# Projecting q and k already transposed, in a two-layer hybrid decoder trunk on one core

## The chip, the cores and the metric

The kernel runs on one NeuronCore of a Trainium2 chip. The metric is device time in microseconds for one execution of the whole program, compared as the median of several executions. The engines are named as the profile names them: PE (TensorE matmul), PEld (its weight loads, which overlap PE), DVE (VectorE), ACT (ScalarE), POOL (GpSimd) and SP (SyncE, which issues the DMAs).

## The reference

Two layers over 512 tokens of width 1024, all in float32. Each layer is

```
h = x + RMSNorm( MixerBlock( RMSNorm(x) ) )
x = h + RMSNorm( ConvGeGLU( RMSNorm(h) ) )
```

One projection `xn @ w_in` feeds three token mixers and their gates. Heads are 64 wide, and the first 16 columns of every q and k head are turned by rotary embedding (column i with column i+8).

- A: dilated window attention, three groups (dilation 1, 4, 16) of 4 heads. Groups 1 and 2 are computed on tokens sorted by residue modulo 4.
- B: 4 heads over the 128 keys that an indexer chooses. The indexer has 8 q heads, one k head and one weight per head: relu(q k), summed with the weights, then top 128 by 16 rounds of eight maxima.
- C: differential attention, 4 heads with two q/k pairs each and values 128 wide.

Each mixer's output is projected to 1024, multiplied by a sigmoid gate, summed, and projected by `w_out`.

## The kernel before, in words

**Numbers.** Every matmul operand is cut into a high and a low part (`split`, line 79: ACT writes the high part, DVE subtracts for the low one), and each product is three matmuls (`mm3`, line 87: lines 88, 89, 90). All weights go through this: `w_emit` (line 112) takes the next unit of a fixed plan, issues its DMAs on SP into a `wr` tile (2 slots) and splits it into `wh` and `wl` (5 slots each). A unit holds at most 1024 elements a partition.

**Order of the work.** `ORDER` (line 44) lists the projection units and gate blocks of a layer. A scheduler orders instructions at compile time by this program order and by its own estimate of time; on the chip each engine runs its list in order. The code lays the attention between the projections by hand: `later(f, lag)` puts a piece of work aside, and `slot()` (line 328) runs what is due, up to two index-score jobs, one step of up to three attention chains in flight (scores, transpose, values), and some steps of top-k. `slot()` is called after each token tile of a projection, and after each gate block.

**The projection unit** (`proj_unit`, line 396) makes q, k and v of two heads (A, B) or of one C head. For each of the four tiles of 128 tokens `proj_tile` (line 370) runs 8 x 3 matmuls: the transposed normed input (`xh`, `xl`, 128 tokens) stands as the weights, and 384 weight columns move (456 in the first unit, which also makes the indexer's k and head weights). Then:

- ACT copies q and k (and v, for groups 1 and 2) out of PSUM into `qr` (line 411);
- DVE applies rotary with four small instructions (`rope`, lines 362 to 365);
- after each second tile PE transposes q and k of two tiles in a group of four transposes (`tqk`, line 437);
- `double_k` (lines 388, 390) and `stack_q` (lines 381 to 384) cut the transposed halves into high and low parts, two heads apart on the partitions, each instruction 64 partitions by 256 tokens;
- v is split out of PSUM. For groups 1 and 2 it goes to DRAM and comes back in residue order (`vr`).

`index_q` (line 705) makes the indexer's q the same way: three tiles, 512 columns moving, four transposes each (line 718). The gate blocks (`branch`, line 752) already stand the weights and move all 512 tokens.

**A layer's start.** The first unit can only project a token tile when `boundary` (line 789) and `pre_norm` (line 221) of the layer before have normed it and PE has transposed it (line 237); the four tiles come one after another.

Of the kernel before, what the change touches and what calls it, by code (L numbers as in the profile page):

```python
# [40 lines left out]
SBUF_SLOTS = dict(u=10, qk=4, v=4, wr=2, wh=5, wl=5, sm=4, pt=4, qr=3, vr=1, th=3, s=24, s1=2, md=4, wi=1, lp=1, q0=2, cw=1)  # L41
# [8 lines left out]
def tile_trunk(ctx, tc, x, positions, w_in, w_br_a, w_br_b, w_br_c, w_out, lam_q1, lam_k1, lam_q2, lam_k2,  # L50
# [88 lines left out]
    def w_ahead(n):  # L139
        w_emit(wnext[0] + n)  # L140
# [5 lines left out]
    unit_cols = {}  # L146
    for g in range(3):
        for p in range(2):
            b = 768 * g + p * P
            unit_cols["A", g, p] = [(b, P), (b + 256, P), (b + 512, P)]  # L150
    unit_cols["A", 0, 0] = unit_cols["A", 0, 0] + [(OFF_I + 512, 72)]
    for h in range(4):
        b = OFF_C + h * P
        unit_cols["C", h] = [(b, P), (b + 512, P), (b + 1024, P)]
    for p in range(2):
        b = OFF_B + p * P
        unit_cols["B", p] = [(b, P), (b + 256, P), (b + 512, P)]
    unit_cols["I"] = [(OFF_I, 512)]
    def plan_unit(l, u):
        cols = unit_cols[u]  # L160
        width = sum(w for _, w in cols)
        for kk in range(4):
            def srcs(rv, kk=kk):
                o = 0
                for c0, w in cols:
                    yield rv[:, :, o:o + w], rows(w_in[l, kk * 256:(kk + 1) * 256, c0:c0 + w])
                    o += w
            w_unit((l, u, kk), [2, width], srcs)
# [17 lines left out]
    def plan_layer(l):  # L186
        for u in ORDER:
            if u[0] in BRANCH:
                plan_branch(l, BRANCH[u[0]], *u[1:])
            else:  # L190
                plan_unit(l, u)
# [120 lines left out]

    xdr = [x[0]] + [dr.tile([S, D], F32, name=f"xd{i}") for i in range(3)] + [out[0]]
    a_scr = [[dr.tile([S, 132], F32, name=f"ascr{l}_{p}") for p in range(2)] for l in range(DEPTH)]
    v_scr = [[[dr.tile([S, P], F32, name=f"vscr{l}_{g}_{p}") for p in range(2)] for g in range(2)] for l in range(DEPTH)]
# [39 lines left out]

    def rope(v, nh, ti):
        t1 = alloc([P, 8, 16], F32, "s1")
        t2 = alloc([P, 8, 16], F32, "s1")
# [18 lines left out]


# [17 lines left out]
    def proj_unit(l, u, perm, nh, idx=None):  # L396


        keys = [(l, u, kk) for kk in range(4)]
        n = sum(w for _, w in unit_cols[u])  # L400
        dv = P // nh
        qkT = alloc([P, 6, S], F32R, "qk")
        v = alloc([P, NT, nh, 2, dv], F32R, "v")
        raws = []
        for t in range(NT):
            units = w_get(keys)
            acc = proj_tile(units, t, n)
            w_ahead(2)
            qr = alloc([P, 384], F32, "qr")
            nq = 384 if perm is not None else 256  # L410
            nc.scalar.copy(qr[:, 0:nq], acc[:, 0:nq])
            if perm is not None:
                nc.sync.dma_start(perm[t * P:(t + 1) * P, :], qr[:, 256:384])
            else:
                vv = acc[:, 256:384].rearrange("p (h d) -> p h d", h=nh)
                split(v[:, t, :, 0, :], v[:, t, :, 1, :], vv)
            nh_r = 4
            if idx is not None:
                nc.scalar.copy(qr[:, 256:320], acc[:, 384:448])
                nc.scalar.activation(idx["w"][:, t, :], acc[:, 448:456], AF.Copy, scale=float(8 ** -0.5))  # L420
                nh_r = 5
            rope(heads(qr[:, 0:nh_r * HD]), nh_r, t)
            if idx is not None:
                nc.vector.tensor_copy(qr[:, 320:384], qr[:, 256:320])
            raws.append(qr)

            def tk(t=t, qr=qr):
                tp = palloc("tp")
                nc.tensor.transpose(tp[:, 0:P], qr[:, 256:384], ident)
                c = slice(t * P, (t + 1) * P)  # L430
                split(idx["k"][:, 0, c], idx["k"][:, 1, c], tp[:, 0:P])

            def tqk(j=t // 2):
                tp = palloc("tp")
                for i in range(2):
                    for w in range(2):
                        nc.tensor.transpose(tp[:, (2 * w + i) * P:(2 * w + i + 1) * P],
                                            raws[2 * j + i][:, w * P:(w + 1) * P], ident)
                if perm is not None:
                    at = lambda i: qkT[:, i].rearrange("p (r i) -> p r i", r=NT)[:, :, j * 64:(j + 1) * 64]  # L440
                    qt, kt = (tp[:, c:c + 256].rearrange("p (i r) -> p r i", r=NT) for c in (0, 256))
                else:
                    at = lambda i: qkT[:, i, j * 256:(j + 1) * 256]
                    qt, kt = tp[:, 0:256], tp[:, 256:512]
                for h in range(2):
                    double_k(at(2 + 2 * h), at(3 + 2 * h), kt, HALF[h])
                stack_q(at(0), at(1), qt)

            if idx is not None:
                later(tk, 2)  # L450
            if t % 2 == 1:
                later(tqk, 2)
            if t < NT - 1:
                slot()
        if perm is not None:
            vr = alloc([P, NT, P], F32, "vr")
            nc.sync.dma_start(vr, perm.rearrange("(i r) c -> i r c", r=NT))

            def tv():
                vv = vr.rearrange("p t (h d) -> p t h d", h=nh)  # L460
                split(v[:, :, :, 0, :], v[:, :, :, 1, :], vv)
            later(tv, 2)
        return qkT, v
# [154 lines left out]

    def chains_b(qkT, v, masks, oTs, i):
# [8 lines left out]
        for parts in PARTS:  # L628
            for h in range(2):
# [17 lines left out]
                def fin():  # L647
# [3 lines left out]
                    to_oT(on, oTs, i)  # L651
# [53 lines left out]
    def index_q(l, qi):  # L705
        keys = [(l, "I", kk) for kk in range(4)]
        for t in range(1, NT):
            units = w_get(keys)
            acc = proj_tile(units, t, 512)
            w_ahead(2)  # L710
            qr = alloc([P, 512], F32, "sm")
            nc.scalar.copy(qr, acc)
            rope(heads(qr), 8, t)

            def go(t=t, qr=qr):
                tp = palloc("tp")
                for b in range(4):
                    nc.tensor.transpose(tp[:, b * P:(b + 1) * P], qr[:, b * P:(b + 1) * P], ident)
                c = slice((t - 1) * P, t * P)
                stack_q(qi[:, 0:8:2, c], qi[:, 1:8:2, c], tp.rearrange("p (b c) -> p b c", b=4))  # L720
            later(go, 2)
            if t < NT - 1:
                slot()
# [89 lines left out]
    for t in range(1, NT):  # L813
        later(first[t], t)
# [225 lines left out]
```

## Time and profile before

| what | us |
|---|---|
| median of 3 runs (1870.73 to 1873.17) | 1872.28 |
| the profiled execution, its own time | 1872.52 |
| its span, first to last instruction | 1870.7 |
| PE busy in it | 1836.4 (98%) |
| DVE busy | 1233.6 (66%) |
| ACT busy | 852.5 (46%) |
| POOL busy | 29.8 (2%) |

The time lies 1.8 us over the span. [...] Layer 0's mixer lies at about 20 to 485 us of the span, its feed-forward part up to about 940 us; layer 1 repeats the pattern.

### The profile page before, as it was taken

Reading aid. Unit: us, or ns where it says so; the run is one execution under the profiler, and the core shown is the slowest. Engines: PE = TensorE matmul, PEld = TensorE weight load, DVE = VectorE, ACT = ScalarE, POOL = GpSimd, SP = SyncE. Lnnn points to the kernel's source line nnn. Section 1 sums busy time; section 2 is a strip of 40 time slices with the busy share of each in tenths; the row PEclk is TensorE's granted clock in tenths of the full one; section 3 lists DMA queues with packets and bytes.
Section 4 is the critical chain, followed back from the end, with each engine's and each line's share of the span. In section 5 each row is a group of like instructions: output and inputs, shape, how many; then the busy total and the mean of one; then the engine's idle time right before and its main releaser. Section 6 shows DMA issues by size and latency. Waiting matters only on the chain.

```text
span 1870.7 us, 26241 instructions
## 1 busy us (share of the span) xinstructions
PE 1836.4 (98%) x9565; PEld 1606.0 (86%) x9565; DVE 1233.6 (66%) x2670; ACT 852.5 (46%) x1668; POOL 29.8 (2%) x53
## 2 busy tenths in 40 slices
PE   7999989999999999999999999899999999999998
PEld 6999979988889888888889999799888898888886
DVE  6798998764546666642378898997645576666332
ACT  5666654453335444432256655545533354444221
POOL 0000000000000000000000000000000000000000
PEclk9999999999999999999999999999999999999999
DMA  5333322232343333323332333232323443332341
GB/s 153 98 80 87 86 74 77 67 105 80 102 151 107 110 105 96 91 101 132 122 113 76 78 100 89 68 80 68 105 81 110 135 136 91 101 102 91 101 149 65
DMA packets 265181, 185.28 MB, mean 99 GB/s; under 512 B 14711, under 2 KB 238299, under 8 KB 265051
## 3 DMA queue, kind: packets, MB, share of 16 engines
q1 hardware_dynamic: 265050, 183.60, 33.5%
q8 instruction: 75, 1.23, 0.3%
q14 instruction: 56, 0.45, 0.1%
HBM read 171.99 MB, written 11.57 MB: 98 GB/s over the span
## 4 chain that ended last, share of the span: by engine, by line
PE 80%; DVE 11%; DMA 3%; issue 2%; ACT 2%; SPq 1%; POOL 0%; DVEq 0%; POOLq 0%; ACTq 0%
PE mm L88 18%; PE mm L89 18%; PE mm L90 18%; PE sc L89 4%; PE sc L88 4%; PE sc L90 4%; PE pv L89 2%; PE pv L88 2%; PE pv L90 2%; DVE wl L82 1%; DVE qk L390 1%; DMA wr<-in_w_in_dram 1%; PE pv L488 1%; PE tp L477 1%; DVE u L746 1%
## 5 line engine op out<-in xcount | busy, mean ns | idle before, releaser
L82 DVE TENSOR_TENSOR wl<-wr,wh 128x1024 fp32r<-128x1024 f32 (+2 forms) x314 | 359.4, 1146 | 351.9 <-ACT wh L81 350.8
L81 ACT CAST wh<-wr 128x1024 fp32r<-128x1024 f32 (+2 forms) x314 | 309.7, 988 | 463.5 <-PE mm L90 135.3
L88 PE MATMUL mm<-xh,wh 128*128 128x512 f32 (+1 forms) x784 | 298.3, 381 | 5.5 <-DVE v L82 4.2
L90 PE MATMUL mm<-xh,wl 128*128 128x512 f32 (+1 forms) x784 | 296.5, 378 | 1.2 <-DVE wl L82 1.2
L89 PE MATMUL mm<-xl,wh 128*128 128x512 f32 (+1 forms) x784 | 296.9, 379 | 0.0
L89 PE MATMUL mm<-wl,xh 128*128 128x384 f32 (+2 forms) x816 | 282.8, 347 | 1.1 <-DVE wl L82 1.1
L88 PE MATMUL mm<-wh,xh 128*128 128x384 f32 (+2 forms) x816 | 281.1, 349 | 2.2 <-ACT wh L81 1.0
L90 PE MATMUL mm<-wh,xl 128*128 128x384 f32 (+2 forms) x816 | 282.6, 347 | 0.0
L88 PEld LDWEIGHTS mm<-xh,wh 128*128 128x128 f32 x784 | 147.8, 188 | 32.8 <-DVE v L82 5.0
L90 PEld LDWEIGHTS mm<-xh,wl 128*128 128x128 f32 x784 | 147.7, 188 | 28.2 <-DVE wl L82 1.6
L89 PEld LDWEIGHTS mm<-xl,wh 128*128 128x128 f32 x784 | 147.8, 188 | 25.9 <-DVE xl L82 0.4
L88 PEld LDWEIGHTS mm<-wh,xh 128*128 128x128 f32 x816 | 153.9, 189 | 8.1 <-ACT xh L81 2.0
L89 PEld LDWEIGHTS mm<-wl,xh 128*128 128x128 f32 x816 | 154.4, 189 | 6.2 <-DVE wl L82 2.5
L90 PEld LDWEIGHTS mm<-wh,xl 128*128 128x128 f32 x816 | 154.3, 189 | 3.9 <-DVE s L226 0.3
L90 PE MATMUL sc<-xh,wl 128*128 128x512 f32 (+1 forms) x272 | 99.3, 365 | 0.0
L89 PE MATMUL sc<-xl,wh 128*128 128x512 f32 (+1 forms) x272 | 99.2, 365 | 0.0
L88 PE MATMUL sc<-xh,wh 128*128 128x512 f32 (+1 forms) x272 | 99.0, 365 | 0.0
L89 PE MATMUL mm<-wl,qk 128*128 128x512 f32 x216 | 85.9, 398 | 0.0
L390 DVE TENSOR_TENSOR qk<-tp,qk 64x256 fp32r<-64x256 f32 x192 | 80.6, 420 | 7.7 <-ACT qk L388 4.8
L88 PE MATMUL mm<-wh,qk 128*128 128x512 f32 x216 | 85.5, 396 | 0.0
L388 ACT CAST qk<-tp 64x256 fp32r<-64x256 f32 x192 | 70.2, 366 | 33.3 <-DVE qk L390 26.1
L90 PE MATMUL mm<-wh,qk 128*128 128x512 f32 x216 | 85.0, 395 | 0.0
(262 smaller groups left out, 3331.7 us busy)
## 6 DMA issues: line engine op xcount, KB each, us to landing
wr<-in_w_ffn_up_dram SPq DMA_DIRECT2D x176, 256.0 KB, 3.4
wr<-in_w_in_dram SPq DMA_DIRECT2D x282, 128.0 KB, 2.4
wr<-in_w_in_dram SPq DMA_DIRECT2D x56, 512.0 KB, 3.8
wr<-in_w_ffn_down_dram SPq DMA_DIRECT2D x44, 512.0 KB, 3.7
wr<-in_w_out_dram SPq DMA_DIRECT2D x16, 512.0 KB, 3.6
xd<-u SPq DMA_DIRECT2D x12, 512.0 KB, 3.1
u<-xd SPq DMA_DIRECT2D x12, 512.0 KB, 6.3
u<-in_x_dram SPq DMA_DIRECT2D x8, 512.0 KB, 6.1
```

The source lines that it names most:

```text
L81: nc.scalar.copy(hi, src)
L82: nc.vector.tensor_tensor(lo, src, hi.bitcast(F32), op=ALU.subtract)
L88: nc.tensor.matmul(dst, a[0], b[0], start=start, stop=False)
L89: nc.tensor.matmul(dst, a[0], b[1], start=False, stop=False)
L90: nc.tensor.matmul(dst, a[1], b[0], start=False, stop=stop)
L388: nc.scalar.copy(kh[o], src[r])
L390: nc.vector.tensor_tensor(kl[o], src[r], kh[r].bitcast(F32), op=ALU.subtract)
L477: nc.tensor.transpose(tp[:, b * P:(b + 1) * P], e[:, b * P:(b + 1) * P], ident)
L488: nc.tensor.matmul(dst, pT[0][:, c], v, start=i == 0, stop=False)
L746: nc.vector.match_replace(out=w, in_to_replace=m8, in_values=w, imm_value=MARK)
```

## The change

- q and k of a unit, and the indexer's q, are made by `proj_block`: a weight block of 128 columns stands, and all 512 tokens move (384 for the indexer's q). The result is already transposed, so lines 437 and 718 go, and with them `qr` and nearly all of `rope`.
- Rotary is done on the transposed result: ACT copies PSUM to `raw`, DVE shuffles partitions within groups of 32 into `swp`, and POOL multiplies `raw` and `swp` by cosine and signed sine tables (two instructions) and adds them (a third). The two tables are built once, with eight transposes.
- `stack_q` and `double_k` now read `raw` from SBUF, 64 partitions by 512 tokens.
- v is projected for many heads at once, in four units: V0 (group 0 of A, with the indexer's k and weights, 328 columns), V1 (groups 1 and 2, 512), V2 (all of C, 512), V3 (B, 256). V1 and V2 are written to DRAM, and each unit loads its 128 columns of it back through `vr` (one slot).
- `ORDER` is new. The eight gate blocks of A come after C1, where before four came after C2 and four after C3.
- `slot()` is called by matmul columns done (`beat`: every 18 x 512), also inside blocks and gate blocks; V units call it once a tile.
- B's final transposes are held back until the last gate blocks. The large `u` tiles have 9 slots, not 10.

The core of the diff:

```diff
-SBUF_SLOTS = dict(u=10, qk=4, v=4, wr=2, wh=5, wl=5, sm=4, pt=4, qr=3, vr=1, ...)
+SBUF_SLOTS = dict(u=9, m1=1, qk=4, v=4, wr=2, wh=5, wl=5, sm=4, pt=4, rp=4, vr=1, ..., kr=2)
-ORDER = [("A", 0, 0), "I", ("A", 1, 0), ("A", 2, 0), ("A", 0, 1), ("A", 1, 1), ("A", 2, 1), ("C", 0), ("C", 1),
-         ("C", 2), ("ga", 0, 4), ("C", 3), ("ga", 4, 8), ("B", 0), ("B", 1), ("gc", 0, 8), ("gb", 0, 8)]
+ORDER = [("V", 0), "I", ("A", 0, 0), ("A", 0, 1), ("V", 1), ("A", 1, 0), ("A", 2, 0), ("A", 1, 1), ("A", 2, 1),
+         ("V", 2), ("C", 0), ("C", 1), ("ga", 0, 8), ("C", 2), ("C", 3), ("V", 3), ("B", 0), ("B", 1),
+         ("gc", 0, 8), ("gb", 0, 8)]
+BEAT = 18 * 512
+    def beat(n):
+        beats[0] += n
+        while beats[0] >= BEAT:
+            beats[0] -= BEAT
+            slot()
+    def proj_block(key, c0=0):
+        w, = w_get([key])
+        n = S - c0
+        acc = palloc("mm")
+        for k in range(KT):
+            mm3(acc[:, 0:n], (w[0][:, k], w[1][:, k]), (xh[:, k, c0:S], xl[:, k, c0:S]), k == 0, k == KT - 1)
+            if k < KT - 1:
+                beat(3 * n)
+        w_ahead(1)
+        raw = alloc([P, S], F32, "rp")
+        swp = alloc([P, S], F32, "rp")
+        nc.scalar.copy(raw[:, 0:n], acc[:, 0:n])
+        nc.vector.stream_shuffle(swp[:, 0:n], raw[:, 0:n], swap)
+        nc.gpsimd.tensor_tensor(raw[:, 0:n], raw[:, 0:n], rot[0][:, c0:S], op=ALU.mult)
+        nc.gpsimd.tensor_tensor(swp[:, 0:n], swp[:, 0:n], rot[1][:, c0:S], op=ALU.mult)
+        nc.gpsimd.tensor_tensor(raw[:, 0:n], raw[:, 0:n], swp[:, 0:n], op=ALU.add)
+        return raw[:, 0:n], 3 * n
-    def proj_unit(l, u, perm, nh, idx=None):
...
+    def v_unit(l, i, vts=None, idx=None):
+        n = sum(w for _, w in v_cols[i])
+        for t in range(NT):
+            acc = proj_tile(w_get([(l, "V", i, kk) for kk in range(4)]), t, n)
+            w_ahead(2)
+            if vts is None:
+                st = alloc([P, S], F32, "rp")
+                nc.scalar.copy(st, acc)
+                nc.sync.dma_start(v_scr[l][i - 1][t * P:(t + 1) * P, :], st)
+            else:
+                for p in range(2):
+                    vv = acc[:, p * P:(p + 1) * P].rearrange("p (h d) -> p h d", h=2)
+                    split(vts[p][:, t, :, 0, :], vts[p][:, t, :, 1, :], vv)
...
+            slot()
+    def qk_unit(l, u, residues=False):
...
+        raw, n = proj_block((l, u, 0))
+        later(lambda raw=raw: stack_q(at(0), at(1), by(raw)))
+        beat(n)
+        raw, n = proj_block((l, u, 1))
+        def dk(raw=raw):
+            for h in range(2):
+                double_k(at(2 + 2 * h), at(3 + 2 * h), by(raw), HALF[h])
+        later(dk)
+        beat(n)
+        return qkT
+    def v_load(l, i, c0, nh):
+        v = v_tile(nh)
+        vr = alloc([P, NT, P], F32, "vr")
...
+        later(tv, 2)
     def index_q(l, qi):
-        for t in range(1, NT):
...
+        for b in range(4):
+            raw, n = proj_block((l, "I", b), P)
+            later(lambda b=b, raw=raw: stack_q(qi[:, 2 * b], qi[:, 2 * b + 1], raw))
+            beat(n)
-                    to_oT(on, oTs, i)
+                    held.append(lambda: to_oT(on, oTs, i))
```

## Rows read from the trace of the kernel before

**Rows 1.** The page: busy us (share, instructions), then DVE busy tenths in 40 slices.

```profile
PE 1836.4 (98%) x9565; PEld 1606.0 (86%) x9565; DVE 1233.6 (66%) x2670; ACT 852.5 (46%) x1668; POOL 29.8 (2%) x53
...
DVE  6798998764546666642378898997645576666332
```

**Rows 2.** The chain that ended last, share of the span by engine.

```profile
PE 80%; DVE 11%; DMA 3%; issue 2%; ACT 2%; SPq 1%; POOL 0%; DVEq 0%; POOLq 0%; ACTq 0%
```

**Rows 3.** Two stretches of layer 0's mixer: us, then each engine's busy us.

```profile
20.00:400.00 380.00, 371.14 (x2186) 346.00 (x2185) 324.52 (x954) 220.12 (x537) 5.44 (x5) 1.00 0.32 82
160.00:250.00 90.00, 88.65 (x562) 85.33 (x561) 82.59 (x264) 52.95 (x139) 0.00 (x0) 1.00 0.32 85
```

**Rows 4.** Timeline of PE around one group of transposes: start us, us, instruction.

```profile
40.28 0.37 PE L90 MATMUL mm<-wh,xl 128*128 128x456 f32 x1
40.49 0.37 PE L88 MATMUL mm<-wh,xh 128*128 128x456 f32 x1
40.70 0.60 PE L437 MATMUL tp<-ident,qr 128*128 128x128 f32 x4
41.05 0.45 PE L89 MATMUL mm<-wl,xh 128*128 128x456 f32 x1
41.34 0.36 PE L90 MATMUL mm<-wh,xl 128*128 128x456 f32 x1
```

**Rows 5.** Groups of transposes by line: count, duration ns min/median/max.

```profile
L437 PE MATMUL tp<-ident,qr x192: 269/273/422, 40.7 to 1322.4; 128*128 128x128 f32 x192
...
L718 PE MATMUL tp<-ident,sm x24: 270/272/296, 58.4 to 995.6; 128*128 128x128 f32 x24
```

**Rows 6.** Timeline of PE: first and last of 7 wide and of 11 narrower matmuls.

```profile
56.64 0.39 PE L90 MATMUL mm<-wh,xl 128*128 128x512 f32 x1
...
58.01 0.40 PE L90 MATMUL mm<-wh,xl 128*128 128x512 f32 x1
...
59.12 0.34 PE L88 MATMUL mm<-wh,xh 128*128 128x384 f32 x1
...
60.86 0.33 PE L89 MATMUL mm<-wl,xh 128*128 128x384 f32 x1
```

**Rows 7.** Timeline of PE at layer 1's start: idle us before, and what ended it.

```profile
952.49 0.47 PE L88 MATMUL mm<-wh,xh 128*128 128x456 f32 x1 [0.25 <-ACT xh L81]
959.22 0.48 PE L88 MATMUL mm<-wh,xh 128*128 128x456 f32 x1 [0.25 <-ACT xh L81]
```

**Rows 8.** Timeline of PE at the first gate blocks of A, layer 0.

```profile
261.29 0.51 PE L88 MATMUL mm<-xh,wh 128*128 128x512 f32 x1 [2.60 <-DVE v L82]
269.55 0.38 PE L488 MATMUL pv<-v,pt 128*128 128x256 f32 x1 [0.82 <-ACT pt L81]
271.24 0.55 PE L477 MATMUL tp<-ident,sm 128*128 128x128 f32 x3 [1.30 <-DVE u L85]
```

**Rows 9.** DVE groups by line and shape: busy us, mean ns of one, idle before.

```profile
L390 DVE TENSOR_TENSOR qk<-tp,qk 64x256 fp32r<-64x256 f32 x192 | 80.6, 420 | 7.7 <-ACT qk L388 4.8
...
L384 DVE TENSOR_TENSOR qk<-tp,qk 64x256 fp32r<-64x256 f32 x48 | 20.4, 426 | 0.9
L383 DVE TENSOR_TENSOR qk<-tp,qk 64x256 fp32r<-64x256 f32 x48 | 20.0, 417 | 4.2 <-ACT qk L382 2.8
L362 DVE TENSOR_TENSOR s<-qr,cc 128x64 f32<-128x64 f32 x88 | 19.3, 219 | 14.0 <-ACT qr L411 13.5
...
L363 DVE TENSOR_TENSOR s<-qr,nsn 128x32 f32<-128x32 f32 x88 | 16.3, 185 | 0.0
...
L781 DVE COPY u<-mm 128x512 f32<-128x512 f32 x12 | 8.3, 691 | 16.0 <-ACT sm L780 16.0
```

**Rows 10.** POOL groups by line and shape: busy us, mean ns of one.

```profile
L256 POOL MEMSET cmask<- 128x512 bf16 x1 | 0.5, 524 | 0.0
...
masks.py:199 POOL TENSOR_SCALAR_AFFINE_SELECT ident<-ident 128x128 f32<-128x128 f32 x1 | 0.3, 292 | 0.0
```

**Rows 11.** Timeline of DVE, 295 to 298 us.

```profile
295.29 1.22 DVE L82 TENSOR_TENSOR wl<-wr,wh 128x1024 fp32r<-128x1024 f32 x1
296.43 0.69 DVE L745 MAX8 s<-u 128x8 f32<-128x512 f32 x1
```

**Rows 12.** Timeline of POOL, the same instruction at two places.

```profile
295.52 1.86 POOL L94 TENSOR_TENSOR s<-s,nhalf 128x4 f32<-128x4 f32 x1 [29.48 <-DVE s L697]
...
325.74 1.01 POOL L94 TENSOR_TENSOR s<-s,nhalf 128x4 f32<-128x4 f32 x1 [28.36 <-DVE s L697]
```

More of the change, by code (lines that the diff above doesn't have):

```diff
@@ L167, in srcs, with plan_qk @@
                     o += w
-            w_unit((l, u, kk), [2, width], srcs)
+            w_unit((l, "V", i, kk), [2, width], srcs)
+    def plan_qk(l, u):
+        for b, col in enumerate(qk_cols[u]):
+            def srcs(rv, col=col):
+                yield rv, rows(w_in[l, :, col:col + P])
+            w_unit((l, u, b), [KT, P], srcs)
     def plan_branch(l, gi, c0, c1):
@@ L394, in score_mm @@
         nc.tensor.matmul(dst, q, kl, start=False, stop=True)
-    def proj_unit(l, u, perm, nh, idx=None):
-        keys = [(l, u, kk) for kk in range(4)]
-        n = sum(w for _, w in unit_cols[u])
-        dv = P // nh
-        qkT = alloc([P, 6, S], F32R, "qk")
[L403 to L463, printed above, removed]
@@ new lines, in v_tile, with tk @@
+    def v_tile(nh):
+        return alloc([P, NT, nh, 2, P // nh], F32R, "v")
+    def v_unit(l, i, vts=None, idx=None):
+        n = sum(w for _, w in v_cols[i])
+        for t in range(NT):
+            acc = proj_tile(w_get([(l, "V", i, kk) for kk in range(4)]), t, n)
[8 more added lines that the diff above has]
+                    split(vts[p][:, t, :, 0, :], vts[p][:, t, :, 1, :], vv)
+            if idx is not None:
+                kr = alloc([P, P], F32, "kr")
+                nc.scalar.copy(kr[:, 0:HD], acc[:, 256:320])
+                nc.scalar.activation(idx["w"][:, t, :], acc[:, 320:328], AF.Copy, scale=float(8 ** -0.5))
+                rope(heads(kr[:, 0:HD]), 1, t)
+                nc.vector.tensor_copy(kr[:, HD:P], kr[:, 0:HD])
+                def tk(t=t, kr=kr):
+                    tp = palloc("tp")
+                    nc.tensor.transpose(tp[:, 0:P], kr, ident)
+                    c = slice(t * P, (t + 1) * P)
+                    split(idx["k"][:, 0, c], idx["k"][:, 1, c], tp[:, 0:P])
+                later(tk, 2)
+            slot()
@@ L814, in tile_trunk @@
         later(first[t], t)
+    later(rotary_rows, 2)
     for l in range(DEPTH):
@@ L861, in tile_trunk @@
                 later(lambda: index_scores(qi, idx["k"], idx["w"], masks), 3)
+            elif u[0] == "V":
+                if u[1] in (0, 3):
+                    vts[u[1]] = [v_tile(2) for _ in range(2)]
+                v_unit(l, u[1], vts.get(u[1]), idx if u[1] == 0 else None)
             elif u[0] == "A":
                 g, p = u[1], u[2]
-                qkT, v = proj_unit(l, u, v_scr[l][g - 1][p] if g > 0 else None, 2, idx if u == ("A", 0, 0) else None)
+                qkT = qk_unit(l, u, g > 0)
+                v = v_load(l, 0, 256 * (g - 1) + p * P, 2) if g > 0 else vts[0][p]
                 if g == 0:
```

95 lines of the change are left out of this document (55 added, 40 removed).

## The prediction

> **What bounds the kernel now.** I read the page first. PE is busy for 98% of the span, DVE for 66%, and DVE's slices show that its share is no average worth using: it is 0.7 to 0.9 in the first eight slices, which are layer 0's mixer, and again from slice 21 on [rows 1]. The chain that ended last lies on PE for 80% of the span and on DVE for 11% [rows 2]. So PE work that goes away is gained almost whole, wherever DVE doesn't step into its place. The stretches say how close that is: from 20 to 400 us PE is idle for 9 us of 380 and DVE for 55.5, and from 160 to 250 us DVE has 7.4 us left of 90 [rows 3]. Two limits lie close together there: PE binds, and DVE could.
>
> **PE: the transposes.** A transpose's recorded 273 ns is no price, since records overlap; the distance between starts is. Around one group of four, matmuls of 456 columns start 0.21 us apart; after the matmul at 40.49 the second next would start at 40.91, and it starts at 41.34 [rows 4]. A group costs 0.43 us. There are 192 transposes of q and k and 24 of the indexer's q [rows 5], that is 54 groups: 54 x 0.43 = 23.2 us. The tables add two groups, 0.9 us.
>
> **PE: wider matmuls.** The columns that move are the same before and after; their number per matmul isn't. Seven matmuls of 512 columns start 1.37 us apart from first to last, 0.228 us each; eleven of 384 take 1.74 us, 0.174 each [rows 6]. That is 0.00042 us a column, and by this line 328 columns take 0.150 and 256 take 0.120. Before, from the loops: 2112 of 384, 192 of 456 and 144 of 512 columns, 367.5 + 40.3 + 32.8 = 440.6 us. After: 1536 of 512, 192 of 384, 192 of 328 and 192 of 256, 350.2 + 33.4 + 28.8 + 23.0 = 435.4 us. That is 5.2 us less. Together with the transposes PE loses 23.2 - 0.9 + 5.2 = 27.5 us.
>
> **A layer's start.** At layer 1's start PE waits for token tiles as they are normed: it idles 0.25 us for `xh` at 952.49 and at 959.22, and the last tile's date is set by DVE, not by PE [rows 7]. Before, three tiles of the first unit, 24 x 0.21 = 5.0 us each, fill the time until the fourth. V0's tile is narrower, 24 x 0.150 = 3.6 us, and nothing else is ready, since the next blocks want all tokens. Three tiles fill 4.2 us less, and that PE stands idle: +4.2 in layer 1, and I take half, +2.1, in layer 0, where loads and not norms set the date. Bounds 0 and 8.4. One `u` slot fewer could make the residual's tile load later; I take 0 for that, since the slots are freed at the pace of the same norms, with 3 us as its bound.
>
> **DVE.** Rotary goes: the instructions of lines 362 and 363, and 365 and 364, which have their shapes and are taken at their price, 88 x 2 x (0.219 + 0.185) = 71 us, with 80.6 + 20.4 + 20.0 us of low parts [rows 9], 192 us in all. Back come 48 shuffles, 96 low parts of k and 48 of q, all 512 wide. The shuffle isn't in this trace; the nearest row, a copy of 128x512, takes 0.69 us [rows 9], and I take it for all three: 192 x 0.69 = 132 us. If the shuffle took twice that, it would be 33 us more. The relief is 60 us, 30 a layer; small instructions overlap their neighbours more than long ones, so I count 25. With the 55.5 us that are free [rows 3], DVE has about 80 us a layer to give. The indexer and C's values come out about even.
>
> **ACT** keeps a like amount: copies of 512 columns for copies of 256, and half as many high parts twice as wide. It is half idle in the stretch [rows 3], so I cost it at nothing. The same holds for SP: one weight DMA a block in place of three a quarter unit, of the same bytes. The load of `vr` is issued behind weights that are several units ahead, and `vr` has one slot, whose former reader is due two slots after its own load and the next load more than five slots later; so no weight DMA should wait behind it.
>
> **POOL.** 28 blocks a layer bring 84 instructions of 512 columns with two inputs. No such instruction is in the trace. The nearest below is a memset of 512 columns, 0.52 us; the nearest that reads is a select on 128 float32 columns, 0.29 us, four times which is 1.17 [rows 10]. Two inputs read in turn would double that, 2.3 us. I take 1.2, by the row that reads, and keep 0.52 and 2.3 as ends. Three of them are 3.6 us, against 24 x 0.228 = 5.5 us of PE for a block: POOL keeps up, with four `rp` buffers and three PSUM banks between. [...]
>
> **What POOL and DVE share.** The same POOL instruction takes 1.01 us at 325.74 and 1.86 us at 295.52; at the second place DVE was inside `wl<-wr,wh`, which reads two SBUF tensors, from 295.29 to 296.51, and POOL ended 0.87 us after that [rows 11, 12]. POOL waits for a DVE instruction of this kind. Whether DVE waits for POOL the trace doesn't show, since POOL's instructions here read 4 columns or fewer. The bounds of what one POOL instruction costs DVE are 0 and its whole length, 1.2 us. I take half, 0.6, because DVE often has an instruction with a PSUM input or one input next: 84 x 0.6 = 50 us a layer, within the 80. In the tightest stretch it is just hidden, so I add 2 us a layer for waits that leak, +4.
>
> **The sum.** Against the profiled execution's 1872.5 us (the median of the runs, 1872.28, is the same): 1872.5 - 27.5 + 6.3 + 4 = 1855 us.
>
> **Rivals.** *Slower: the shared read side makes DVE the bound.* If DVE stands still for each POOL instruction's whole 1.2 us, a layer loses 84 x 1.2 = 101 us against 80 free, 21 us over, 42 in both layers: 1855 - 4 + 42 = 1893 us. DVE becomes the bound from 0.95 us lost an instruction, and the kernel is slower than before from 1.08 (21 us of net gain used up). For it: the wait at 295.52 and DVE's 82.6 of 90 us [rows 3, 12]. Against: much of DVE's work there, top-k and masked scores, has one SBUF input. [...]
>
> *The wait for A grows.* At the first gate blocks of A PE idles 2.60, 0.82 and 1.30 us, on DVE and ACT [rows 8]: A's combined output isn't there yet. Before, 12 slots of projection lie between A's last unit and these gates; now V2 gives 4 and C0 and C1 give 5.3. The 2.7 missing slots are worth 18 x 0.228 = 4.1 us each, 22 us in both layers at most; gate products that need no A output can fill about half. That gives 1855 + 11 = 1866, at worst 1877. My sum has 0 here, as DVE's relief pulls the other way.
>
> *Faster still.* If DVE's relief counts and POOL's share costs nothing, those 4.7 us of waits a layer go, and the leak with them: 1855 - 9.4 - 4 = 1842.
>
> That the transposes stay in another form I exclude: the diff leaves no PE instruction in their place.
>
> **Chances.** About 0.2%, 3.7 us, is what a measurement of this kernel can tell from no change, so faster means below 1868.5 and slower above 1876. The forecast, with 1846 to 1864 as its own range, 0.50; the wait for A, 1864 to 1878, 0.17, half of it faster and a third within; DVE as the bound, 0.20, with its low edge (0.02) within and the rest slower; faster still, 0.13. Faster: 0.50 + 0.13 + 0.08 = 0.71; within 0.2%: 0.06 + 0.02 = 0.08; slower: the rest, 0.21. The range of 8 in 10 leaves out the upper half of DVE as the bound and the lower half of the fastest case: 1840 to 1890.
>
> **What would show it.** Right: no group at lines 437 and 718's place, projections as 512-column matmuls 0.228 us apart, about 168 more POOL instructions of 1 to 1.5 us, DVE busy 40 to 60 us less in sum, a few microseconds of idle PE on `xh` at layer 1's start. Wrong: DVE instructions with two SBUF inputs grown well over 0.69 and 1.22 us, or PE waits on `wl` and `qk` released by DVE or POOL all through the mixer; or idle PE of more than 15 us a layer before A's gate blocks; or POOL instructions over 1.8 us, whereby three exceed a block.

## The result, and the profile after

The kernel after takes 1939.32 us (median of 4 runs, 1937.12 to 1941.74) against 1872.38 (1870.73 to 1873.17) of the kernel before on the same chip: a ratio of 1.0359, 95% interval 1.0341 to 1.0377. It is slower by 67 us, where 1855 us was forecast; the range ended at 1890. The profiled execution took 1941.74 us, its span is 1940.0.

The page after (busy us, share and instructions; then the tenths of PE's granted clock, of DVE and of POOL; then the chain by engine) answers to [rows 1, 2]:

```profile
PE 1844.7 (95%) x9021; PEld 1543.6 (80%) x9021; DVE 1313.1 (68%) x2232; ACT 856.2 (44%) x1458; POOL 295.9 (15%) x223
...
DVE  5989798885446766642389987988855466666432
...
POOL 1714230340000000000034351204300000000000
PEclk9999989999999999999999999899999999999999
...
PE 66%; DVE 18%; ACT 4%; issue 4%; DMA 4%; POOL 3%; SPq 0%; DVEq 0%; POOLq 0%; ACTq 0%
```

The matmuls have become fewer (9565 to 9021), yet PE's busy sum is longer. DVE has 438 instructions less and 80 us more of busy time. The chain has lost 14 points on PE and gained 7 on DVE and 3 on POOL.

The two stretches of [rows 3] (PE, PEld, DVE, ACT, POOL busy, then the granted clock):

```profile
20.00:400.00 380.00, 349.20 (x1753) 293.65 (x1754) 328.37 (x672) 199.92 (x386) 122.62 (x78) 0.94 0.30 84
160.00:250.00 90.00, 83.29 (x425) 69.27 (x425) 78.07 (x147) 54.58 (x98) 31.64 (x18) 0.92 0.30 86
```

PE idles 31 us of 380 where it idled 9, and its granted clock has fallen from 1.00 to 0.94. DVE is as busy as before with 282 instructions less. Layer 0's feed-forward part loses nothing: from 485 to 970 us PE is busy for 484.4 us of 485 at a granted clock of 1.00. So the loss lies in the mixers, and instructions have grown. Which ones, the groups of DVE and POOL show (busy us, mean ns); they answer to [rows 9, 10]:

```profile
L85 DVE TENSOR_TENSOR wl<-wr,wh 128x1024 fp32r<-128x1024 f32 x284 | 356.9, 1258 | 322.0 <-ACT wh L84 321.2
L441 DVE TENSOR_TENSOR qk<-rp,qk 64x512 fp32r<-64x512 f32 x96 | 106.2, 1106 | 13.8 <-ACT qk L439 12.7
L435 DVE TENSOR_TENSOR qk<-rp,qk 64x512 fp32r<-64x512 f32 x24 | 37.1, 1544 | 0.8
L423 DVE STREAM_SHUFFLE rp<-rp 128x512 f32<-128x512 f32 x48 | 35.3, 735 | 0.1
```

```profile
L425 POOL TENSOR_TENSOR rp<-rp,rot 128x512 f32<-128x512 f32 x48 | 82.2, 1713 | 0.0
L424 POOL TENSOR_TENSOR rp<-rp,rot 128x512 f32<-128x512 f32 x48 | 77.8, 1622 | 365.2 <-DVE rp L423 365.2
L426 POOL TENSOR_TENSOR rp<-rp,rp 128x512 f32<-128x512 f32 x48 | 73.7, 1536 | 3.6
```

The shuffle is nearly as priced, 0.735 for 0.69. The low parts of q and k are not: 1.11 and 1.54 us. The timelines show how. First POOL, then DVE, from 60 to 68 us (start, us, instruction); they answer to [rows 11, 12]:

```profile
60.35 1.01 POOL L424 TENSOR_TENSOR rp<-rp,rot 128x384 f32<-128x384 f32 x1
61.32 2.00 POOL L425 TENSOR_TENSOR rp<-rp,rot 128x384 f32<-128x384 f32 x1
63.40 1.21 POOL L426 TENSOR_TENSOR rp<-rp,rp 128x384 f32<-128x384 f32 x1
```

```profile
60.45 1.99 DVE L85 TENSOR_TENSOR wl<-wr,wh 128x1024 fp32r<-128x1024 f32 x1 [0.21 <-ACT wh L84]
62.48 1.26 DVE L434 TENSOR_TENSOR qk<-rp,qk 64x384 fp32r<-64x384 f32 x1
63.77 1.26 DVE L435 TENSOR_TENSOR qk<-rp,qk 64x384 fp32r<-64x384 f32 x1
65.06 1.22 DVE L85 TENSOR_TENSOR wl<-wr,wh 128x1024 fp32r<-128x1024 f32 x1
...
66.83 0.55 DVE L434 TENSOR_TENSOR qk<-rp,qk 64x384 fp32r<-64x384 f32 x1
```

Read them as turns. `wl` begins at 60.45 inside L424, which ends at 61.36, and ends 1.08 us after that. L425, begun at 61.32, ends at 63.32, 0.88 us after `wl` has let go at 62.44. L434, begun at 62.48, ends 0.42 us after L425. At 65.06, with POOL idle, `wl` takes 1.22 us, and at 66.83, just ahead of POOL's next instruction, L434 takes 0.55. In these turns each engine waits for the end of the other's instruction: before, the trace showed POOL's side alone [rows 11, 12].

PE waits for DVE's steps of attention (lines 519 and 731), up to 8.9 us at once; the longest wait at A's gates was 2.60 before [rows 8] (engine, line, released by: us in total, times, longest):

```profile
PE sc L444 <- DVE s L519: 15.9, 8, 8.9
PE sc L444 <- DVE md L519: 11.2, 7, 4.4
...
PE tp L526 <- DVE sm L731: 7.4, 4, 4.9
```

and so do the lists behind POOL:

```profile
ACT qk L439 <- POOL rp L426: 50.3, 19, 6.0
ACT qk L432 <- POOL rp L426: 35.7, 21, 3.9
```

### The profile page after: what moved, and what is told of

It is laid out like the page before. It is cut to its first block, busy times and chain, and to the rows that moved or that the text cites. A ratio compares the mean times of both kernels' runs of the same rounds, so it can differ in the third digit from the quotient of the medians.

```text
span 1940.0 us, 24034 instructions
## 1 busy us (share of the span) xinstructions
PE 1844.7 (95%) x9021; PEld 1543.6 (80%) x9021; DVE 1313.1 (68%) x2232; ACT 856.2 (44%) x1458; POOL 295.9 (15%) x223
## 4 chain that ended last, share of the span: by engine, by line
PE 66%; DVE 18%; ACT 4%; issue 4%; DMA 4%; POOL 3%; SPq 0%; DVEq 0%; POOLq 0%; ACTq 0%
PE mm L91 15%; PE mm L92 15%; PE mm L93 15%; PE sc L92 4%; PE sc L91 4%; PE sc L93 4%; DVE qk L441 3%; DVE wl L85 2%; DMA wr<-in_w_in_dram 2%; PE pv L92 2%; PE pv L91 2%; PE pv L93 2%; DVE rp L423 1%; DVE sm L519 1%; DVE qk L435 1%
## 5 line engine op out<-in xcount | busy, mean ns | idle before, releaser
L85 DVE TENSOR_TENSOR wl<-wr,wh 128x1024 fp32r<-128x1024 f32 (+2 forms) x298 | 369.0, 1239 | 345.4 <-ACT wh L84 344.6
L91 PE MATMUL mm<-xh,wh 128*128 128x512 f32 (+2 forms) x1232 | 473.2, 384 | 1.9 <-ACT xh L84 1.0
L93 PE MATMUL mm<-xh,wl 128*128 128x512 f32 (+2 forms) x1232 | 472.5, 384 | 0.0
L92 PE MATMUL mm<-xl,wh 128*128 128x512 f32 (+2 forms) x1232 | 471.9, 383 | 0.0
L91 PEld LDWEIGHTS mm<-xh,wh 128*128 128x128 f32 x1232 | 233.6, 190 | 43.0 <-ACT xh L84 1.4
L93 PEld LDWEIGHTS mm<-xh,wl 128*128 128x128 f32 x1232 | 233.5, 190 | 40.6
L424 POOL TENSOR_TENSOR rp<-rp,rot 128x512 f32<-128x512 f32 (+1 forms) x56 | 88.4, 1579 | 406.5 <-DVE rp L423 387.3
L441 DVE TENSOR_TENSOR qk<-rp,qk 64x512 fp32r<-64x512 f32 x96 | 106.2, 1106 | 13.8 <-ACT qk L439 12.7
L425 POOL TENSOR_TENSOR rp<-rp,rot 128x512 f32<-128x512 f32 (+1 forms) x56 | 94.9, 1694 | 0.0
L93 PE MATMUL mm<-wh,xl 128*128 128x512 f32 (+2 forms) x256 | 92.8, 364 | 2.0 <-DVE xl L85 2.0
L91 PE MATMUL mm<-wh,xh 128*128 128x512 f32 (+2 forms) x256 | 92.5, 362 | 1.6 <-ACT xh L84 1.6
L92 PE MATMUL mm<-wl,xh 128*128 128x512 f32 (+2 forms) x256 | 91.2, 357 | 1.5 <-DVE wl L85 1.5
L426 POOL TENSOR_TENSOR rp<-rp,rp 128x512 f32<-128x512 f32 (+1 forms) x56 | 85.7, 1531 | 4.2
```

Of the source, the lines that this page charges most:

```text
L85: nc.vector.tensor_tensor(lo, src, hi.bitcast(F32), op=ALU.subtract)
L91: nc.tensor.matmul(dst, a[0], b[0], start=start, stop=False)
L92: nc.tensor.matmul(dst, a[0], b[1], start=False, stop=False)
L93: nc.tensor.matmul(dst, a[1], b[0], start=False, stop=stop)
L424: nc.gpsimd.tensor_tensor(raw[:, 0:n], raw[:, 0:n], rot[0][:, c0:S], op=ALU.mult)
L425: nc.gpsimd.tensor_tensor(swp[:, 0:n], swp[:, 0:n], rot[1][:, c0:S], op=ALU.mult)
```

## The experiments

Each time is that of a single run, but for the last two kernels. It is compared with the kernel before on the same chip (1871.9 to 1875.6 us); "over before" is that difference, and of differences under 4 us, the 0.2% of the prediction, nothing is made. Theory 1: GpSimd's instructions that read SBUF and DVE's with two SBUF inputs hold each other up. Theory 2: GpSimd's chain is long, and what waits for it costs the time. Theory 3: the new order of units leaves too little ahead of A's gates.

**The turning left out** (x1): no shuffle, no GpSimd instructions.

```diff
-        swp = alloc([P, S], F32, "rp")
-        nc.vector.stream_shuffle(...)
-        nc.gpsimd.tensor_tensor(...)   # three
```

> Leaves out the rotary turn of q, k and the indexer's q (shuffle and the three GpSimd instructions of each block); all else as changed. Changed kernel: 1939 us. Theory 1 (GpSimd and DVE shut each other out of SBUF's shared read side): DVE loses 37 us of shuffles and some 80 us by which its two-SBUF-input instructions are stretched, and the time falls to 1845 to 1865, the forecast's 1855 or better. Theory 2 (not the sharing, but three long GpSimd instructions in a row, for which ACT and DVE wait at the head of their lists): the same, 1845 to 1865, so this run only tells both from theory 3. Theory 3 (the new order of units, the beats and the layer start cost the time): it stays at 1900 or more.

1853.57 us, 19.6 below before. So all else that the change does is worth 20 us, DVE's relief from the old turning included, and the new turning costs 86. Theory 3 falls as the main cause: the order of units is the same. The page of x1:

```profile
PE 1814.8 (98%) x9021; PEld 1529.9 (83%) x9021; DVE 1178.5 (64%) x2120; ACT 856.3 (46%) x1458; POOL 30.2 (2%) x55
```

**GpSimd that only writes** (x2): five integer fills a block in place of the three instructions, the shuffle kept.

```diff
-        nc.gpsimd.tensor_tensor(...)   # three
+        sw = swp[:, 0:n].bitcast(I32)
+        for i in range(5):
+            nc.gpsimd.iota(sw, pattern=[[0, n]], base=1065353216 + i, channel_multiplier=0)
+        raw = swp
```

> Keeps the shuffle, and puts five GpSimd instructions that only write 512 columns (iota) in the place of the three that read; q and k are then constants, so this leaves the rotary turn and the projected values out. The chain from PSUM to the high and low parts stays about as long as before it, an estimated 4 us of GpSimd, and ACT and DVE wait for it in the same places. Theory 1: DVE's two-SBUF-input instructions fall back to their length in the kernel before (0.69 and 1.22 us), and the time falls to 1850 to 1875. Theory 2: nothing that matters has changed, 1920 to 1940. Theory 3: 1920 to 1940 too.

1859.12 us, 14.0 below before, and DVE's lengths are what they are without GpSimd (`wl` takes 1228 ns at most in x1 as here). The rows of `wl` and of the low parts of k in x2 (count: min/median/max ns), then the same of the kernel after:

```profile
L442 DVE TENSOR_TENSOR qk<-rp,qk x96: 661/689/1107, 80.1 to 1308.0; 64x512 fp32r<-64x512 f32 x96
L85 DVE TENSOR_TENSOR wl<-wr,wh x298: 685/1225/1228, 8.6 to 1824.3; 128x1024 fp32r<-128x1024 f32 x142, 128x512 fp32r<-128x512 f32 x4, 128x656 fp32r<-128x656 f32 x3
```

```profile
L441 DVE TENSOR_TENSOR qk<-rp,qk x96: 660/1054/2107, 84.6 to 1389.0; 64x512 fp32r<-64x512 f32 x96
L85 DVE TENSOR_TENSOR wl<-wr,wh x298: 683/1224/2304, 8.5 to 1906.8; 128x1024 fp32r<-128x1024 f32 x142, 128x512 fp32r<-128x512 f32 x4, 128x656 fp32r<-128x656 f32 x3
```

That speaks for theory 1. But five fills take 3.1 us a block, from the first's start to the last's end (median of 56 blocks), and the three instructions 4.9, so theory 2 isn't excluded.

**The kernel before with GpSimd load** (x5): 144 multiplications of 128x512 that read `qr` and the identity and whose result nobody reads.

```diff
             rope(heads(qr[:, 0:nh_r * HD]), nh_r, t)
+            pool_load(qr, 2 if t % 2 else 1)
```

> The kernel before, 1872 us, with 144 more GpSimd multiplications of 512 float32 columns (144 of the change's 168), six a projection unit, that read what the rotary instructions have written and whose results nobody reads. Theory 1: DVE's two-SBUF-input instructions are stretched while GpSimd works, 30 to 80 us of DVE time in sum, and the time grows by 10 to 40 us. Theory 2: nobody waits for these results but the next user of a qr slot, so within 5 us of 1872.

1901.18 us, 28 over before. No instruction of the kernel waits for the added ones but for buffers (3.1 us), and the lists of PE, DVE and ACT are, instruction by instruction, those of the kernel before. So this is contention by itself:

```profile
L371 POOL TENSOR_TENSOR pd<-qr,ident x144: 1269/1295/2290, 34.2 to 1349.9; 128x512 bf16<-128x512 f32 x144
...
L82 DVE TENSOR_TENSOR wl<-wr,wh x314: 937/1225/2171, 9.1 to 1866.4; 128x1024 fp32r<-128x1024 f32 x110, 128x768 fp32r<-128x768 f32 x44, 128x912 fp32r<-128x912 f32 x3
```

The low parts of k, which take one operand from PSUM, stay in this run at the 420 ns that they have before [rows 9]:

```profile
L396 DVE TENSOR_TENSOR qk<-tp,qk 64x256 fp32r<-64x256 f32 x192 | 80.7, 420 | 7.6 <-ACT qk L394 4.7
```

**The gates of A later** (x4): C2 ahead of the first half of A's gates, C3 ahead of the second.

> The changed kernel with A's gate blocks where they stood before: C2 ahead of the first four, C3 ahead of the other four. Theory 3: the waits ahead of A's gates (9.0 us and 5.3 us at one place each) go, and the time falls by 10 to 30 us. Theories 1 and 2: DVE has as much to do and GpSimd too, within 6 us of 1939.

1935.15 us, 4 below the kernel after. The longest wait in the mixers fell from 8.9 to 5.5 us, and PE still waits for the same steps of DVE.

**A longer chain of writes** (x6): nine fills in place of five.

> The run with GpSimd writes only, but with nine written blocks of 128x512 integers a block of q or k in place of five, so that GpSimd's part lasts about as long as in the kernel after (nine at about 0.53 us, 4.8 us, against a mean of 1.62 + 1.71 + 1.54 = 4.9 us). The turning of q and k is left out; q and k are constants. Theory 1 (GpSimd's reads of SBUF and DVE's two-input instructions hold each other up): 1855 to 1872 us, DVE's lengths as before. Theory 2 (what costs is that ACT and DVE wait in order behind a chain of GpSimd of this length, whatever it does): 1905 to 1945 us.

1903.75 us, 30.7 over before, with DVE's lengths as in x2 (`wl` 1228 ns at most). Theory 1 alone doesn't give that; it is just below what theory 2 wanted. The run also showed a flaw of all these pairs: the compile-time scheduler orders every kernel anew, and x6's lists differ from x2's. GpSimd also falls further behind than nine fills for five would make it: counted in order, every ninth fill ends 9.3 us after its shuffle by the median, in p3 below, with as many fills, 5.5.

**The turning on DVE** (x3), **one GpSimd instruction a block** (x7), **all four steps on DVE out of PSUM** (x8).

```diff
-        nc.gpsimd.tensor_tensor(...)   # three
+        nc.vector.tensor_tensor(...)   # three
```

> The three elementwise instructions of the turning run on DVE in place of GpSimd; nothing else changes. They are some 168 instructions of 128x512 more on DVE, at about 0.62 us (half of a 128x1024 subtraction) 104 us, so DVE's busy sum should come to about 1320 us, what it is in the kernel after. Theory 1 (GpSimd and DVE holding each other up is the cost): 1860 to 1895 us, DVE's lengths as before. Theory 2 (DVE has no room for 80 us more of busy time, whatever makes it): 1915 to 1945 us, as after.

> DVE shuffles and multiplies by the first table straight from PSUM (ACT's copy goes), GpSimd keeps one multiplication a block (56 in place of 168), and DVE adds the two later, ahead of the splits. DVE gets 112 instructions of about 0.62 us more (70 us), a third of GpSimd's reads stays. Theory 1: 1865 to 1905 us, with DVE's long instructions about a third as often lengthened as in the kernel after. Theory 2 (DVE has no room): 1915 to 1945 us.

> All four steps of the turning on DVE, the shuffle and the first multiplication straight from PSUM; ACT's copy goes. DVE's work as in the run with the turning on DVE, ACT has some 56 copies less, PSUM is held until DVE has read it twice. Theory 1: 1860 to 1895 us; within 10 us of the run with the turning on DVE. If the bank of the sum is held too long, PE waits on L407's successor (the sums of the next blocks) and it is above that run. Theory 2: 1915 to 1945 us.

1905.25, 1909.19 and 1902.36 us: 32, 36 and 29 over before. Moving the work to DVE is better than leaving it on GpSimd, by some 35 us, and still worse than before. All three lie between the ranges that theories 1 and 2 gave them. x3's 128 us more on DVE than x1 (1306.9 against 1178.5) come with 52 us more time, though the low parts of k are no longer than in x1 (1093 ns at most, 1099 there). That is not the price of DVE's work alone: in x3 ACT waits 88 us for the end of this chain on DVE, as it waits 86 for GpSimd's in the kernel after. In x7 some of the lengthening is still there (`wl` up to 2310 ns).

**The order held still** (p1 to p4). The lists of PE, DVE and ACT are fixed by ordering dependencies between neighbours, without a semaphore; the traces of p2 and of the kernel after have 24037 and 24034 instructions. "Short order" is the one that the scheduler made for x2.

```diff
+    for e, at in pins.items():
+        for a, b in zip(at, at[1:]):
+            tc.add_manual_dep(ins[b], ins[a].name, mybir.DependencyInfo(
+                mybir.DependencyClass.NoSync, mybir.DependencyReason.DATA), reason="pin")
```

> The scheduler orders each kernel's instructions anew, so the runs so far differ in order too. Here PE's, DVE's and ACT's lists are held in exactly the order of the kernel after; the three GpSimd instructions of a block are replaced by nine that only write (4.8 us, about what the three take there). The turning is left out, q and k are constants. Theory 1 (reads of SBUF on GpSimd and DVE holding each other up): 1855 to 1880 us. Theory 2 (the length of the GpSimd chain): 1925 to 1945 us, as after. Theory 3 (the order that the scheduler made for the kernel after is a bad one, and contention matters little): 1925 to 1945 us too; the next run tells it from theory 2.

> The kernel after, complete, with PE's, DVE's and ACT's lists held in the order that the scheduler made for the run with five writes (1859 us); only the order differs from the kernel after. Theory 3 (order): 1870 to 1895 us. Theories 1 and 2: within 15 us of the kernel after, 1925 to 1950 us.

> Nine writes a block, as in the run with the longer writes (1904 us), but in the order of the run with five (1859 us): only the length of GpSimd's chain differs from that run, 2 us a block. The turning is left out. If the 45 us between those two runs came from the order, 1860 to 1870 us; if from the longer chain as such, 1890 to 1910 us.

> The turning on DVE (1905 us in its own order), with the lists in the order of the run with five writes and DVE's three instructions right behind each shuffle. If order made that run slow: 1865 to 1885 us. If DVE's 110 us of added work did: 1895 to 1915 us.

Measured: p1 1906.52, p2 1929.49, p3 1886.63, p4 1923.23 us; over before 30.9, 53.9, 11.0, 47.6. (Theory 3 is the order of the instructions here.) p2 came out as theories 1 and 2 wanted; p1 and p3 lie between their two ranges, and p4 above both of its. None of the three theories is the whole. With x2 and the kernel after these make a ladder of one step each, over before:

```
x1  no turning                                   -19.6
x2  shuffle, chain of 3.1 us, writes, order S    -14.0    + 5.6  shuffle and a short chain
p3  chain of 4.6 us (median), writes, order S    +11.0    +25.0  a longer chain
p2  the three real instructions, order S         +53.9    +42.9  GpSimd's reads
kernel after, its own order                      +66.9    +13.0  the order
```

In the traces PE's, DVE's and ACT's lists are the same in x2, p3 and p2, and the same in p1 and the kernel after. x1 stands in an order of its own, so the step of 5.6 holds that too. The step from p3 to p2 is not a longer chain: p2's three instructions take 4.74 us by the median, p3's fills 4.61, and ACT waits 64 us for them where it waits 87 in p3. What grows is DVE's sum, 1313.7 us against 1212.4. In the kernel after's own order the reads are worth 66.9 - 30.9 = 36.0 (p1). What the longer chain does at equal order is seen in the waits of p3, of which x2 has 5.5 us (a recorder wraps these kernels' instructions, so that they bear one line, L385):

```profile
ACT qk L385 <- POOL rp L778: 86.6, 31, 5.3
```

ACT stands in its list behind GpSimd, and the high parts of weights and P behind it. In x6, where the scheduler knew of the long chain and put the splits later, ACT waits 5 us, but DVE is busy for only 54.5 us of the first 100 (65.3 in p3, 65.4 in x2), and between 200 and 300 us PE is busy for 85.7 us where x2 has 95.1. The delay is paid in either way. p4 comes nearest to the price of DVE's work alone, as ACT waits little there (8.2 us for the chain): against x2, in whose order PE and ACT stand, its 106 us more on DVE (1319.1 against 1212.8) cost 47.6 + 14.0 = 61.6 us. It is above x3, so with the three instructions right behind each shuffle the same work is worse placed.

**The splits two slots later** (y1), **packed rows** (y2), **packed rows and later splits** (y3), **with SyncE's queue** (y4). Of 128 rows 32 are turned; transfers bring them into tiles of 128x128, where DVE needs a quarter of the columns.

```diff
-        nc.gpsimd.tensor_tensor(...)   # three
+        gather(nc.scalar, nc.scalar, a, b, raw, n)
+        nc.vector.tensor_tensor(a[0:m], a[0:m], rotp[c0 > 0][0][0:m], op=ALU.mult)
+        nc.vector.tensor_tensor(b[0:m], b[0:m], rotp[c0 > 0][1][0:m], op=ALU.mult)
+        nc.vector.tensor_tensor(a[0:m], a[0:m], b[0:m], op=ALU.add)
+        for h in range(2):
+            nc.scalar.dma_start(chunks(raw, 64 * h, 16, n), a[h * m // 2:(h + 1) * m // 2, :])
```

> The kernel after, complete; the splits of q and k that wait for GpSimd's chain are put two slots behind their block in place of one. If ACT and DVE standing in order behind the chain is what the chain's length costs: 1905 to 1925 us, with ACT's waits for GpSimd (86 us in the kernel after) mostly gone. If it is that attention's work comes later, or the contention alone: 1935 to 1965 us.

> The turning without GpSimd and on packed rows: of the 128 rows of a block only 32 are turned; transfers from SBUF to SBUF bring them, cut into four pieces of 128 tokens, into a tile of 128x128 and, with the halves swapped, into a second one; DVE multiplies and adds there (three instructions of 128x128, at about 0.28 us by the like ones on v, 47 us in sum in place of the shuffles' 40), and two transfers bring the result back. All transfers are issued on ACT's queue. Two transfers of 2.7 to 3.8 us by the landing times shown make a chain of about 7 to 9 us. If a longer chain costs as such (27 us for 2 us): 1910 to 1950 us. If only contention and DVE's work mattered: 1855 to 1870 us.

> As the run with packed rows, the splits two slots behind their block in place of one. If engines standing in order behind the chain is its cost: 1855 to 1875 us, and faster than the run with packed rows. If later attention is: slower than it.

> As the run before it, with the transfers of the swapped rows and of the result issued on SyncE's queue, where the weights' loads stand too. If ACT's 400 issues cost it time: a few us faster than the run before; if SyncE's waits for weight buffers hold them up: 10 to 40 us slower.

y1 1944.80, y2 1936.17, y3 1949.45, y4 1910.88 us. y1 doesn't test what it was meant to: ACT's waits for GpSimd stayed (76 us, against 86), since four `rp` buffers allow no more lead, I suppose. y2 and y3 leave GpSimd out of the turning, DVE's sums are near x2's (1216 and 1217 us, 1212.8 there), and both are about as slow as the kernel after. Their transfers are not free to issue; the DMA issues of y2 (count: min/median/max ns):

```profile
L331 ACTq DMA_DIRECT2D pk<-rp x112: 594/607/718, 50.5 to 1369.0; - x112
L333 ACTq DMA_DIRECT2D pk<-rp x112: 688/706/1235, 51.3 to 1369.6; - x112
L334 ACTq DMA_DIRECT2D pk<-rp x112: 688/705/938, 52.6 to 1371.9; - x112
L443 ACTq DMA_DIRECT2D rp<-pk x112: 553/622/1262, 58.4 to 1376.5; - x112
```

Eight issues a block are 5.3 us of ACT's queue, 296 us in sum. With six of the eight on SyncE's queue (y4) it is 39 us faster than y3, where a few us were expected. The latency of the transfers themselves was thus not separated from their issue. y3, 13 us above y2, had a later split that didn't help.

**The gates of A behind all projections** (z1), **and A ahead of the indexer** (z2), both on top of x8.

```diff
-         ("V", 2), ("C", 0), ("C", 1), ("ga", 0, 8), ("C", 2), ("C", 3), ("V", 3), ("B", 0), ("B", 1),
-         ("gc", 0, 8), ("gb", 0, 8)]
+         ("V", 2), ("C", 0), ("C", 1), ("C", 2), ("C", 3), ("V", 3), ("B", 0), ("B", 1),
+         ("ga", 0, 8), ("gc", 0, 8), ("gb", 0, 8)]
```

> The run with the turning on DVE out of PSUM (1902 us), complete, with the gates of A moved behind C's and B's projections, so that five more projections stand between A's attention and the point at which PE must have its result. If PE waits there for DVE's attention work: the stall of 9 us and those beside it go, 1870 to 1888 us. If DVE is simply full over the whole mixer, the stall only moves on: 1895 to 1905 us.

> As the run before it, and A's first q and k ahead of the indexer's, so that attention begins some 20 us earlier in a layer. If DVE's idle time at a layer's start is what is missing later: 5 to 20 us faster than the run before it (1855 to 1880 us). If not, or if the masks of B come late in its place: same or slower than it.

1947.15 us (1945.3 to 1948.6; 1.0392, interval 1.0377 to 1.0408, of before) and 1961.93 (1.0477, 1.0460 to 1.0495): both well slower than x8's 1902, and z1 is above both of its ranges. That PE's stall at A's gates costs the time, as z1 was to show, is not borne out. The windows of z1, then of x8 (columns as above):

```profile
100.00:200.00 100.00, 96.09 (x497) 81.42 (x496) 98.27 (x205) 62.96 (x109) 0.00 (x0) 0.97 0.30 85
200.00:300.00 100.00, 86.48 (x446) 73.58 (x444) 92.44 (x217) 48.85 (x100) 0.00 (x0) 0.91 0.29 80
300.00:350.00 50.00, 47.60 (x244) 39.36 (x243) 49.04 (x109) 25.89 (x51) 2.36 (x2) 1.00 0.35 95
350.00:400.00 50.00, 34.79 (x144) 27.00 (x145) 40.28 (x106) 20.59 (x51) 2.99 (x3) 0.76 0.08 21
```

```profile
300.00:350.00 50.00, 50.00 (x232) 41.61 (x231) 41.80 (x75) 15.71 (x24) 1.01 (x1) 1.00 0.28 74
350.00:400.00 50.00, 49.52 (x292) 43.42 (x290) 47.45 (x111) 30.04 (x65) 0.00 (x0) 1.00 0.36 96
```

From 100 to 300 us DVE is nearly full in z1, as it is in x8 (98.2 and 90.7 us). With the gates out of the way it stays full to 350 us, where x8's DVE has 41.8 us, and at the end PE has nothing left to cover the rest: 34.8 us busy of 50 at a granted clock of 0.76. I read this as the gates in the middle letting DVE catch up.

No version here beats the kernel before while it computes the same; x1 and x2, at 1854 and 1859, leave the turning out.

## Why the prediction was wrong

**PE's gain was nearly right.** 9565 - 9021 = 544 matmul records are gone, the 216 transposes of [rows 5] among them, and x1, which has this gain and not the turning, is 19.6 us faster although it still idles more at the first layer's start. Against 27.5 - 6.3 = 21.2 in the sum that is within 2 us. Some luck is in this: x1's PE is busy for 21.6 us less than before (1814.8 against 1836.4), not 27.5, and x1 also has 55 us less on DVE, which the sum counted at nothing.

**The layers' starts were right in sum, by luck.** From 20 to 50 us PE is busy for 24.2 us where it was busy for 28.5, 4.3 more idle, not 2.1; 2.7 of it is the tables' transposes waiting for DVE at `sm` (L334 <- L331), which I had costed as PE work alone. At layer 1's start [rows 7] PE's waits between 930 us and the first units are 1.7 us instead of 0.9: +0.8, not +4.2. The two errors cancel. The 4.2 went by a date of the last tile that DVE was to set; [rows 7] show waits for ACT's `xh`, of 0.25 us.

**DVE's relief was too large before any contention.** In x2, where nothing lengthens DVE (`wl` 1228 ns at most), its busy sum is 1212.8 us against 1233.6: 21 us, not 60. I took 0.69 us for all low parts. 48 of the 160 low parts of q and k take 1.04 to 1.13 us in x1 and x2: those of the eight units whose tokens are put in order of residues, six each, which now read SBUF in strides. That is 18 of the 39 us. Another part is the turning that goes: taken out of the trace before, its four lines shorten DVE's busy sum by 45 us, not 71, since the small instructions overlap their neighbours (at 89.92 us line 362 takes 0.22 us, and line 363 starts 0.14 us after it did).

**The step that failed is the price of what POOL and DVE share: "half, 0.6 ... 84 x 0.6 = 50 us a layer, within the 80. In the tightest stretch it is just hidden", so "+4".** The bounds, 0 and the whole instruction, were right to be kept. DVE does wait: at 60.45 us `wl` took 1.99 us for 1.22, and GpSimd's L425 behind it 2.00 for 1.01. The turns from 60 to 64 us show the wait on both sides. Beside GpSimd instructions that only write DVE doesn't wait: in x2 `wl` takes 1228 ns at most, as before. The step priced +4; the reads alone cost 36 to 43 us, and the length of POOL's chain, put at nothing by "POOL keeps up", another 25. Four things went wrong in it.

First, the loss: DVE's sum is 1313.1 - 1212.8 = 100 us longer than in x2, 0.60 us an instruction of 168. The 0.6 came out, but it was a half taken for want of a row, and more than half of the loss lies on instructions that the prediction had not thought of (the fourth point); that is luck.

Second, the "80 us a layer" to hide it in. 15 of them came from the overrated relief (25 counted a layer, 10 in x2), and the rest wasn't free. 55.5 us of idle DVE between 20 and 400 us isn't room for more work wherever it falls: p4 adds 106 us of DVE work to x2, without GpSimd's reads, and pays 62, x3 adds 128 to x1 and pays 52 with ACT's waits. DVE runs its list in order (the same in the traces of x2, p3 and p2), and each idle stretch has a date; work added ahead of attention's steps delays them. z1's 98.3 us of 100 show how near DVE is to being the bound there.

Third, POOL's own side. An instruction of 1.2 us was priced; at its shortest it takes 1.28 (1.27 in x5), with DVE beside it 1.54 to 1.71 on the mean. (That POOL's instructions before read 4 columns or fewer overlooked the select of 128 in [rows 10]; no term rests on it.) The chain became 4.9 us in place of 3.6. I compared it with a block's 5.5 us of PE and found that POOL keeps up. That is throughput. Nobody's wait for the chain's end was costed, although ACT and DVE stand behind it in their lists: at equal order 1.5 us more of chain cost 25 us.

Fourth, the new low parts read q and k from SBUF, where the old ones read PSUM [rows 9]. I moved them as if only their width had changed; they joined the instructions with two SBUF inputs, and more than half of the loss lies on them: all low parts of q and k together take 180.6 us against 126.3 in x2, line 441's 106.2 against 78.2 among them. With PSUM as one source they lost nothing to GpSimd (420 ns before, 420 in x5). `wl`, the larger group by far, loses 11.5 us (369.0 against 357.5).

**The rivals.** "The shared read side makes DVE the bound" had DVE standing still for GpSimd's reads, and the side, at 0.20, and 1893 us for a loss of 1.2 us an instruction. At the 0.6 that was measured it predicts no loss at all, so its time was reached by other terms: 36 to 43 us from the reads, 25 from the chain, 13 from the order. "The wait for A grows" has a wait in its place: 8.9 us among layer 1's gate blocks of A. But it is a wait for a softmax step of C (line 519), which comes late on DVE, and not for A's output. Nor is it caused by missing slots, as x1 has the same slots without it and x4 gains 4 us by giving some back. PE's clock wasn't in the sum either: the same 9021 matmuls took 1844.7 us busy in the kernel after and 1814.8 in x1, at a granted clock of 0.979 and 0.995 over the span; of the 88 us between the two spans 30 are this longer busy time and 58 idle PE. In the kernel after PE was busy for 8.2 us of the 10 from 264 to 274 us; from 274 to 291 the granted clock was 0.51.

**What stays open.** Each step of the ladder rests on one run, and the steps depend on each other: the reads are worth 43 us in one order and 36 in the other. How the 25 us of the longer chain divide between ACT's waits and later attention: y1 didn't remove the waits. Whether the packed rows would beat the kernel before if fewer transfers were issued.

## What to carry to other kernels

Before work that reads SBUF is moved to GpSimd, list which DVE instructions have two SBUF inputs after the change, not before it, and count the waits on both sides (100 us more on DVE here; 4.9 us for GpSimd's chain, where 3.6 was counted). Don't count an in-order engine's idle time as room for work that others wait behind (62 us lost for 106 added in p4); a chain across engines costs by its length and by what stands behind it in each list, even where its throughput suffices (25 us here). Where a compiler orders the instructions, hold the order still before two variants are compared: it made up to 20 us here (p1 against p3).

## What the runs showed of the hardware that I had not expected

- DVE and GpSimd hold each other up in both directions: a 128x1024 subtraction on DVE that takes 1.22 us in x2 took up to 2.30 in the kernel after, a 128x512 instruction on GpSimd 1.27 at least (x5) and up to 2.31 (the kernel after).
- A DVE subtraction with one operand in PSUM keeps its length beside GpSimd's reads: 420 ns before, 420 in x5.
- GpSimd's fills, which read nothing, leave DVE's lengths as they are (1228 ns at most) at 0.56 us each.
- A split that reads 64x512 in strides of four elements takes 1.07 us, one that reads them in a row 0.69 (x2).
- A transfer from SBUF to SBUF occupies the queue that issues it for 0.57 to 0.71 us by the medians of y2 and y4, on ACT's queue as on SyncE's.
